# Expert weights in slots of two row blocks of four experts, instead of one expert per slot

## The chip, the cores and the metric

The kernel runs on one core of a Trainium2 chip. The metric is the device time of one execution in microseconds (us). Times inside an execution come from a hardware profile of one execution and count from its first instruction.

## The reference

One decoder layer over 256 tokens of width 1024: four token mixers (attention, indexer attention, gated linear attention, RWKV-7) merged by gates, a layer norm, and a mixture of 32 experts in 4 groups, two experts for each token. The part that the change touches is the mixture:

```python
hg = jnp.einsum('sd,edh->seh', xs, w_gate)     # w_gate, w_up: 32 x 1024 x 256
hu = jnp.einsum('sd,edh->seh', xs, w_up)
h = jax.nn.silu(hg) * hu * gate[..., None]     # gate is 0 but for two experts of a token
return jnp.einsum('seh,ehd->sd', h, w_down)    # w_down: 32 x 256 x 1024
x = _layer_norm(DN_ALPHA * x + y, ln_g[l, 1], ln_b[l, 1])
```

All of it is float32. The three expert matrices are 96 loads of 1 MB.

## The kernel before

The layer is one program, unrolled. Its first part (mixers, merge, output projection, router) is written as generators, and the string `ORDER` says by hand, letter by letter, which generator takes its next step. Letters of its last stretch: `O` output projection, `Q` and `R` norm and router of token blocks 0 and 1, `Y` and `Z` their normalised rows, `E` the gather for the first experts, `L` one weight load. Each engine runs its instructions in the order in which the program issues them.

The experts are worked in 8 groups of four (`g`, NQUAD = 8). Up to 32 tokens of each expert are gathered by a matmul with a selection matrix, so that four experts with 32 columns each fill the 128 columns of TensorE. For a group: gate products (`mwg`), `way_back` (two transposes of the selection matrix), up products (`mwu`), gather for the next group (`ahead`), SiLU on ScalarE and VectorE (`hh`), two transposes (`ph`, copied to `hT`), down products (`down`, from `mwd`), a copy to SBUF (`dn_copy`), and `back`, which adds the rows into the four accumulators `yacc` of PSUM. Groups 6 and 7 do their down products at the end of the program, as their `mwd` comes last in `stream`.

All loads go through the queue of SyncE in the order of `stream`: for groups 0 to 5 four `mwg`, four `mwu`, four `mwd`; then `mwg` and `mwu` of 6 and 7; then `mwd` of 6 and of 7. A load (`fetch`) takes a slot of 8 KB in each of 128 partitions, in a cycle of NL = 25 (two of each 25 are made of two half slots, with two loads of half the size). The first 25 are issued by the letters `L`, the others where `wload` first asks for them, and each waits on SyncE until its slot is free. In the kernel before, a slot holds one expert's whole matrix: `[P, 8 row blocks, 256]` for gate and up, `[P, 2, 1024]` for down. The product loop runs over row blocks `k` outside and the four experts inside, so that it touches all four slots from its first step to its last. A float32 matmul here shows as two MATMUL instructions.

The last 8 loads (`mwd` of 6 and 7) are cut: group 6 into row halves of 512 KB, group 7 into pieces of 256 KB by column half and row half (`tails`). At the end the gain and bias rows of the second layer norm are spread over all partitions by matmuls (`spread`, 32 instructions) between the two halves of the down products of group 6; then come `down` of 7, `last_copy`, `last_back`, the moments, the norm, and four stores.

If a token overflows an expert's 32 places (`flag`), a branch at the end computes everything densely; it is jumped over here.

Of the kernel before, what the change touches and what calls it, by code (L numbers as in the profile page):

```python
# [113 lines left out]
def _layout(inp):  # L114
# [35 lines left out]
    o["wout"] = g["w_out"][0].reshape(KT // 2, 2, P, D).transpose(0, 2, 1, 3)  # L150
    o["mwg"] = g["moe_w_gate"][0].reshape(NEXP, KT, P, HID).transpose(0, 2, 1, 3)
    o["mwu"] = g["moe_w_up"][0].reshape(NEXP, KT, P, HID).transpose(0, 2, 1, 3)
    o["mwd"] = g["moe_w_down"][0].reshape(NEXP, 2, P, D).transpose(0, 2, 1, 3)
    pc = np.zeros((P, NPC), f)
# [66 lines left out]
    "CPSMPSCMCDPLDPPPSMCSPSMNPSMPPNPSPCMMNMPMPSNSPCXLLMSMMMNNPPMPLMSPMMSMSMLPLPPMLNMLSPPMSSNPMSMMPMNMMPSS"  # L221
    "PPLLSPPMMMMMMMMPNSMPPMMSUUUUPUUPPMMMOUULMMMMLMMLOUMUMLOUUOUULLLMOUUOULUOQOOQQQQQQQRQQLQQOQLQLRRRYQQQ"
    "QQRSYLRQRRUQRRRRQRRZQZRQRRRRERLRRRRLLREQEQEREL"
)


def body(ctx, tc, I, out):
# [16 lines left out]
    def slot(name, shape, dt=F32):  # L244

        n = int(np.prod(shape[1:]))
        if n > 1024:
            return view(rp.tile([P, 2048], dt, tag="w2", bufs=NW, name=name), n, shape)
        return view(rp.tile([P, 1024], dt, tag="w", bufs=NS, name=name), n, shape)
# [997 lines left out]
    for g in range(NQUAD + 1):  # L1247
        if g < NQUAD:
            stream += [(src, 4 * g + e, [P, KT, HID]) for src in ("mwg", "mwu") for e in range(4)]

        if g != NQUAD - 2:
            for j in ((NQUAD - 2, NQUAD - 1) if g == NQUAD else (g,) if g < NQUAD - 2 else ()):
                stream += [("mwd", 4 * j + e, [P, 2, D]) for e in range(4)]
    fetched, tails = [], []

    def fetch():
        n = len(fetched)
        src, e, shape = stream[n]
        cyc = n % NL
        if cyc >= NL - NS // 2:  # L1260

            m = shape[1] // 2
            h = [slot("w", [P, m, shape[2]]) for _ in range(2)]
            ds = [(h[i], I[src][e][:, m * i:m * i + m]) for i in range(2)]
            at = lambda k: h[k // m][:, k % m]
        else:
            t = view((MP["rb"] if cyc < NR else rp).tile([P, 2048], F32, tag="w2", bufs=NR if cyc < NR else NW, name="w2"), 2048, shape)
            ds = [(t, I[src][e])]
            at = lambda k: t[:, k]
        fetched.append(at)  # L1270
        if n < len(stream) - 8:
            for d, a in ds:
                SY.dma_start(d, a)
            return

        tails.extend((k, at(k), I[src][e][:, k]) for k in range(2))
        if n % 4 == 3:
            for hs in (slice(0, 512), slice(512, 1024)) if n == len(stream) - 1 else (slice(0, 1024),):
                for _, d, a in sorted(tails, key=lambda x: x[0]):
                    SY.dma_start(d[:, hs], a[:, hs])  # L1280
            tails.clear()

# [255 lines left out]
    def down(g, k, h, pd):  # L1538
        for e4 in range(4):
            T.matmul(pd[h][32 * e4:32 * e4 + 32], lhsT=outs[g][0][:, k, 32 * e4:32 * e4 + 32], rhs=wds[g][e4](k)[:, 512 * h:512 * h + 512],  # L1540
                     start=k == 0, stop=k == 1, tile_position=(0, 32 * e4))
# [14 lines left out]
    def back(g, h, dn):  # L1556
        for q in range(2):
            T.matmul(yacc[q, h], lhsT=outs[g][1][:, q], rhs=dn[h], start=False, stop=False, skip_group_check=True)  # L1558

    idA = sq_([P, P], "idA", bufs=1)  # L1560
    G.tensor_scalar(idA, ident, ALPHA, None, op0=OP.mult)
    for g in range(NQUAD):
# [4 lines left out]
        for i, src in enumerate(("mwg", "mwu")):  # L1567
            ws = [wload() for _ in range(4)]
            for k in range(KT):
                for e4 in range(4):  # L1570
                    T.matmul(pgu[32 * e4:32 * e4 + 32, i], lhsT=xg[:, k, 32 * e4:32 * e4 + 32], rhs=ws[e4](k),  # L1571
                             start=k == 0, stop=k == KT - 1, tile_position=(0, 32 * e4))
            if i == 0:
                SGT = way_back(g)
                if more:
                    for q in range(2):
                        select(g + 1, q)
# [14 lines left out]
        V.scalar_tensor_tensor(hh, in0=hh, scalar=1.0, in1=pgu[:, 0], op0=OP.add, op1=OP.mult)  # L1592
        V.scalar_tensor_tensor(hh, in0=hh, scalar=0.5, in1=pgu[:, 1], op0=OP.mult, op1=OP.mult)
        ph = ps([P, 2, P])
        for k in range(2):
# [16 lines left out]
        if g < NQUAD - 2:  # L1612
            pd = downs(g)
            for k in range(2):
                for h in range(2):
                    down(g, k, h, pd)
# [34 lines left out]
    def scaled(q, h, src, dst):  # L1651

        hs = slice(512 * h, 512 * h + 512)
        V.scalar_tensor_tensor(dst[:, hs], in0=src, scalar=mvs[q][:, 0:1], in1=g2[:, hs], op0=OP.subtract, op1=OP.mult)  # L1654

    def normed(q, h, dst):
        hs = slice(512 * h, 512 * h + 512)
        V.scalar_tensor_tensor(dst[:, hs], in0=dst[:, hs], scalar=mvs[q][:, 2:3], in1=b2[:, hs], op0=OP.mult, op1=OP.add)  # L1658
        SY.dma_start(out[128 * q:128 * q + 128, hs], dst[:, hs])
# [3 lines left out]
    pd = downs(g)  # L1663
    for k in range(2):
        for h in range(2):
            down(g, k, h, pd)
        if k == 0:

            g2, b2 = twin("ln2", [P, D])
            for i, t in (("ln_g2", g2), ("ln_b2", b2)):  # L1670
                for h in range(2):
                    p = ps([P, 512])
                    spread(i, h, False, p)
                    A.copy(t[:, 512 * h:512 * h + 512], p)
    for h in range(2):
        dn_copy(dn, pd, h)
    for h in range(2):
        back(g, h, dn)
# [3 lines left out]
    def last_copy(h):  # L1682
        A.copy(dn[h], pd[h])
# [12 lines left out]
    for h in range(2):  # L1696
        down(g, 0, h, pd)
        if h:
            for q in range(2):
                first_half(q)  # L1700
        down(g, 1, h, pd)
        last_copy(h)
    for q in range(2):
# [8 lines left out]
    A.activation(res[0][:, h0], yacc[0, 0], AF.Identity, scale=mv[:, 2:3], bias=mv[:, 3:4])  # L1712
    G.tensor_tensor(res[0][:, h0], res[0][:, h0], g2[:, h0], op=OP.mult)
    G.tensor_tensor(res[0][:, h0], res[0][:, h0], b2[:, h0], op=OP.add)
    scaled(0, 1, yacc[0, 1], res[0])
# [11 lines left out]
    with tc.If(flag > 0):  # L1727
# [8 lines left out]
        for k in range(KT):  # L1736
# [3 lines left out]
            A.activation(xo[k // 4][:, k % 4, :], f2(pt), AF.Identity, scale=pcol("ln_g", k), bias=pcol("ln_b", k))  # L1740
        with tc.For_i(0, NEXP, 1) as e:
            wg, wu, wd_ = (slot("wo", sh) for sh in ([P, KT, HID], [P, KT, HID], [P, 2, D]))
            for t, n in ((wg, "mwg"), (wu, "mwu"), (wd_, "mwd")):
                SY.dma_start(t, I[n][bass.ds(e, 1)][0])
            hx = slot("hx", [P, 2, S])
            pg = ps([P, 2, S])
            pu2 = ps([P, 2, S])
            for c in range(2):
                for k in range(KT):
                    T.matmul(pg[:, c], lhsT=wg[:, k, 128 * c:128 * c + 128], rhs=xo[k // 4][:, k % 4, :], start=k == 0, stop=k == KT - 1)  # L1750
            for c in range(2):
                for k in range(KT):
                    T.matmul(pu2[:, c], lhsT=wu[:, k, 128 * c:128 * c + 128], rhs=xo[k // 4][:, k % 4, :], start=k == 0, stop=k == KT - 1)
            A.activation(hx, pg, AF.Tanh, scale=0.5)
            V.scalar_tensor_tensor(f2(hx), in0=f2(hx), scalar=1.0, in1=f2(pg), op0=OP.add, op1=OP.mult)
            V.scalar_tensor_tensor(f2(hx), in0=f2(hx), scalar=0.5, in1=f2(pu2), op0=OP.mult, op1=OP.mult)
            for q in range(2):
                for h in range(2):
                    pd_ = ps([P, 512], pj)
                    for k in range(2):  # L1760
                        T.matmul(pd_, lhsT=hx[:, k, 128 * q:128 * q + 128], rhs=wd_[:, k, 512 * h:512 * h + 512], start=k == 0, stop=k == 1)
                    hs = slice(512 * h, 512 * h + 512)
                    V.scalar_tensor_tensor(acc[q][:, hs], in0=pd_, scalar=gcur[:, q, 0:1], in1=acc[q][:, hs], op0=OP.mult, op1=OP.add)
            gtmp = sq_([P, 2, 32], "gtmp")
            V.tensor_copy(gtmp[:, :, 0:31], gcur[:, :, 1:32])
            V.tensor_copy(gcur[:, :, 0:31], gtmp[:, :, 0:31])
        for q in range(2):
# [22 lines left out]
```

## Time and profile before

| | us |
|---|---|
| median of 3 runs | 500.91 |
| lowest and highest of the 3 | 498.99, 501.34 |
| profiled execution, its own time | 499.01 |
| its span, first to last instruction | 497.2 |

The span is 1.8 us shorter than the time of the same execution. In it TensorE's matmuls are busy for 454.9 us (91%), VectorE for 237.7 us, ScalarE for 192.2 us, and the queue of SyncE moves 146.11 MB. Matmuls are pipelined and counted from start to modelled end, so "busy" is not peak. PE is TensorE's matmuls, PEld its weight loads, DVE VectorE, ACT ScalarE, POOL GpSimd, SPq the queue of SyncE. L1571 is line 1571 of the kernel. A row "x64" merges 64 instructions. PEclk is the granted share of TensorE's full clock (1.00 is 2.4 GHz, 0.50 is 1.2 GHz).

### The profile page before, as it was taken

The page shows a single profiled execution, that of the slowest core. Times are in us where ns is not written, and L with a number is a line of the kernel's source. Part 1 is how long each engine was busy: PE and PEld are TensorE (multiplying, and loading weights), DVE is VectorE, ACT ScalarE, POOL GpSimd, SP SyncE. Part 2 cuts the span into 40 slices and gives each one's busy share as a digit, 9 for nine tenths or more (in the row PEclk, how much of TensorE's full clock was granted, in tenths as well). Part 3 has the DMA queues.
Part 4 walks back from the last instruction along what each step waited for, and adds up shares of the span by engine and source line. Part 5 has one row for each costly group of instructions (what it writes and reads, how often), then busy time and mean ns, then how long its engine had stood idle before and what let it go on. Part 6 is the DMA issues. An engine that isn't in the chain of part 4 may idle for free. (4 is left out here: it accounts for less than half of the span.)

```text
span 497.2 us, 9471 instructions
## 1 busy us (share of the span) xinstructions
PE 454.9 (91%) x3968; PEld 333.9 (67%) x3968; DVE 237.7 (48%) x487; ACT 192.2 (39%) x353; POOL 49.9 (10%) x52
## 2 busy tenths in 40 slices
PE   7999999999999999999999899998988989876891
PEld 5989898998777888888878776563544536352520
DVE  4568648988987556657664643021212212120015
ACT  5767656353684965344453341010202012010311
POOL 1101112510100004333050000000000000000002
PEclk8899999999999999999999989999999999998897
DMA  8977522222242256699999999999999999999942
GB/s 275 395 330 272 196 86 87 86 88 86 86 171 86 86 181 225 266 426 420 356 407 390 354 371 421 420 397 424 415 420 422 418 422 415 421 420 415 394 170 88
DMA packets 27557, 146.74 MB, mean 295 GB/s; under 512 B 3124, under 2 KB 5752, under 8 KB 12536
## 3 DMA queue, kind: packets, MB, share of 16 engines
q1 hardware_dynamic: 27512, 146.11, 74.7%
q8 instruction: 32, 0.52, 0.4%
q14 instruction: 13, 0.11, 0.1%
HBM read 143.48 MB, written 2.62 MB: 294 GB/s over the span
## 5 line engine op out<-in xcount | busy, mean ns | idle before, releaser
L374 DVE TENSOR_TENSOR hl<-w,hl 128x1024 fp32r<-128x1024 f32 (+1 forms) x75 | 90.3, 1221 | 41.3 <-ACT hl L373 41.3
L373 ACT CAST hl<-w 128x1024 fp32r<-128x1024 f32 (+1 forms) x75 | 74.1, 1014 | 19.8 <-PE ps L390 12.4
L1571 PE MATMUL ps<-w,xg 128*32 128x256 f32 x1024 | 65.6, 396 | 7.6 <-DMA w<-mwu 5.8
L388 PE MATMUL ps<-hl,xh 128*128 128x512 f32 (+1 forms) x160 | 60.3, 377 | 0.0
L390 PE MATMUL ps<-hl,xh 128*128 128x512 f32 (+1 forms) x160 | 58.9, 368 | 0.0
L389 PE MATMUL ps<-hl,xl 128*128 128x512 f32 (+1 forms) x160 | 58.9, 368 | 0.0
L1571 PEld LDWEIGHTS ps<-w,xg 128*32 128x32 f32 x1024 | 33.7, 114 | 37.2 <-issue 8.5
L388 PE MATMUL ps<-xl,hl 128*128 128x256 f32 x160 | 48.7, 304 | 2.9 <-ACT hl L373 2.3
L389 PE MATMUL ps<-xh,hl 128*128 128x256 f32 x160 | 46.9, 293 | 0.1
L390 PE MATMUL ps<-xh,hl 128*128 128x256 f32 x160 | 46.4, 290 | 0.0
L388 PEld LDWEIGHTS ps<-xl,hl 128*128 128x128 f32 x160 | 32.0, 200 | 6.4 <-ACT hl L373 2.5
L1473 PE MATMUL ps<-Sel,nrm 128*128 128x128 f32 x256 | 33.6, 287 | 1.2 <-DVE smr L1437 0.7
L1473 PEld LDWEIGHTS ps<-Sel,nrm 128*128 128x128 f32 x256 | 31.3, 200 | 4.3 <-issue 3.7
L388 PEld LDWEIGHTS ps<-hl,xh 128*128 128x128 f32 x160 | 30.1, 188 | 5.7 <-issue 0.6
L390 PEld LDWEIGHTS ps<-hl,xh 128*128 128x128 f32 x160 | 30.1, 188 | 5.1
L389 PEld LDWEIGHTS ps<-hl,xl 128*128 128x128 f32 x160 | 30.2, 189 | 5.0 <-issue 0.2
L389 PEld LDWEIGHTS ps<-xh,hl 128*128 128x128 f32 x160 | 31.9, 199 | 0.9 <-DVE hl L374 0.7
L1558 PE MATMUL ps<-small,SGT 128*128 128x512 f32 x48 | 23.7, 616 | 9.3 <-DVE small L1552 5.1
L390 PEld LDWEIGHTS ps<-xh,hl 128*128 128x128 f32 x160 | 31.9, 199 | 0.0
L1523 ACT COPY SGT<-ps 128x256 f32<-128x256 f32 x8 | 3.0, 373 | 69.0 <-PE ps L1521 69.0
L1552 DVE COPY small<-ps 128x512 f32<-128x512 f32 x6 | 4.2, 692 | 51.4 <-PE ps L1558 51.4
L1540 PE MATMUL ps<-w,small 128*32 128x512 f32 x192 | 23.1, 598 | 3.5 <-ACT xg L1480 3.0
(405 smaller groups left out, 667.1 us busy)
## 6 DMA issues: line engine op xcount, KB each, us to landing
w<-mwu SPq DMA_DIRECT2D x32, 1024.0 KB, 15.0
w<-mwg SPq DMA_DIRECT2D x27, 1024.0 KB, 15.2
w<-win SPq DMA_DIRECT2D x26, 1024.0 KB, 7.0
w<-mwd SPq DMA_DIRECT2D x23, 1024.0 KB, 14.2
w<-mwd SPq DMA_DIRECT2D x10, 512.0 KB, 13.7
w<-mwg SPq DMA_DIRECT2D x10, 512.0 KB, 15.4
w<-wbr SPq DMA_DIRECT2D x4, 1024.0 KB, 5.7
w<-wout SPq DMA_DIRECT2D x4, 1024.0 KB, 7.4
```

Source lines behind the costliest of these rows:

```text
L373: A.copy(hi, src)
L374: V.tensor_tensor(lo, src, hi.bitcast(F32), op=OP.subtract)
L388: T.matmul(dst, lhsT=ls[0], rhs=rs[1], start=start, stop=False)
L389: T.matmul(dst, lhsT=ls[1], rhs=rs[0], start=False, stop=False)
L390: T.matmul(dst, lhsT=ls[0], rhs=rs[0], start=False, stop=stop)
L1473: T.matmul(pg[:, k4], lhsT=nrm[q][:, 128 * k:128 * k + 128], rhs=f2(SelR[g, q]), start=q == 0 and k4 == 0, stop=True, skip_group_check=True)
L1523: A.copy(SGT, pg)
L1540: T.matmul(pd[h][32 * e4:32 * e4 + 32], lhsT=outs[g][0][:, k, 32 * e4:32 * e4 + 32], rhs=wds[g][e4](k)[:, 512 * h:512 * h + 512], start=k ...
L1552: V.tensor_copy(dn[h], pd[h])
L1558: T.matmul(yacc[q, h], lhsT=outs[g][1][:, q], rhs=dn[h], start=False, stop=False, skip_group_check=True)
L1571: T.matmul(pgu[32 * e4:32 * e4 + 32, i], lhsT=xg[:, k, 32 * e4:32 * e4 + 32], rhs=ws[e4](k), start=k == 0, stop=k == KT - 1, tile_position ...
```

## The change

A slot of gate or up weights now holds two of the eight row blocks of all four experts of a group (`[P, 2, 4, 256]`), and a slot of down weights one row block and one column half of all four experts (`[P, 4, 512]`, slot number 2 h + k). The host lays the arrays out so that a slot is still 8 KB in one piece for each partition. The product loop asks for a new slot with each second `k`. The cut of the last 8 loads is gone: they are whole slots. The down products run by column half `h` first, then `k`, with copy and `back` after each column half for groups 6 and 7. The spread of the gain rows moves into group 7, between its SiLU and its transposes; that of the bias rows comes after the first of four down steps of group 6. The end of `ORDER` is rewritten from its 572nd letter on. The overflow branch goes over four experts in one turn of its loop.

```diff
-    o["mwg"] = g["moe_w_gate"][0].reshape(NEXP, KT, P, HID).transpose(0, 2, 1, 3)
-    o["mwu"] = g["moe_w_up"][0].reshape(NEXP, KT, P, HID).transpose(0, 2, 1, 3)
-    o["mwd"] = g["moe_w_down"][0].reshape(NEXP, 2, P, D).transpose(0, 2, 1, 3)
+    for n, k in (("mwg", "moe_w_gate"), ("mwu", "moe_w_up")):
+        o[n] = g[k][0].reshape(NQUAD, 4, 4, 2, P, HID).transpose(0, 2, 4, 3, 1, 5).reshape(NEXP, P, 2, 4, HID)
+    o["mwd"] = g["moe_w_down"][0].reshape(NQUAD, 4, 2, P, 2, 512).transpose(0, 4, 2, 3, 1, 5).reshape(NEXP, P, 4, 512)
...
-    "PPLLSPPMMMMMMMMPNSMPPMMSUUUUPUUPPMMMOUULMMMMLMMLOUMUMLOUUOUULLLMOUUOULUOQOOQQQQQQQRQQLQQOQLQLRRRYQQQ"
-    "QQRSYLRQRRUQRRRRQRRZQZRQRRRRERLRRRRLLREQEQEREL"
+    "PPLLSPPMMMMMMMMPNSMPPMMSUUUUPUUPPMMMOUULMMMMLMMLOUMUMLOUUOUULLLMOUUOULULOQLOOQQQQOQQRQQQQQRRRQRRRSQY"
+    "LRQRQRQRRQQYRZQLLQQQRRQELZRRRRLRRURLRRQEERRQEE"
...
-        if n < len(stream) - 8:
-            for d, a in ds:
-                SY.dma_start(d, a)
-            return
-
-        tails.extend((k, at(k), I[src][e][:, k]) for k in range(2))
-        if n % 4 == 3:
-            for hs in (slice(0, 512), slice(512, 1024)) if n == len(stream) - 1 else (slice(0, 1024),):
-                for _, d, a in sorted(tails, key=lambda x: x[0]):
-                    SY.dma_start(d[:, hs], a[:, hs])
-            tails.clear()
+        for d, a in ds:
+            SY.dma_start(d, a)
...
-            T.matmul(pd[h][32 * e4:32 * e4 + 32], lhsT=outs[g][0][:, k, 32 * e4:32 * e4 + 32], rhs=wds[g][e4](k)[:, 512 * h:512 * h + 512],
+            T.matmul(pd[h][32 * e4:32 * e4 + 32], lhsT=outs[g][0][:, k, 32 * e4:32 * e4 + 32], rhs=wds[g][2 * h + k](e4),
...
+    gb = []
+
+    def ln2(i, pool):
+
+        if not gb:
+            gb.extend(twin("ln2", [P, D]))
+        for h in range(2):
+            p = ps([P, 512], pool)
+            spread(("ln_g2", "ln_b2")[i], h, False, p)
+            A.copy(gb[i][:, 512 * h:512 * h + 512], p)
...
-            ws = [wload() for _ in range(4)]
             for k in range(KT):
+                if k % 2 == 0:
+                    w = wload()
                 for e4 in range(4):
-                    T.matmul(pgu[32 * e4:32 * e4 + 32, i], lhsT=xg[:, k, 32 * e4:32 * e4 + 32], rhs=ws[e4](k),
+                    T.matmul(pgu[32 * e4:32 * e4 + 32, i], lhsT=xg[:, k, 32 * e4:32 * e4 + 32], rhs=w(k % 2)[:, e4],
...
+        if not more:
+            ln2(0, pj)
         ph = ps([P, 2, P])
...
-    for k in range(2):
-        for h in range(2):
-            down(g, k, h, pd)
-        if k == 0:
-
-            g2, b2 = twin("ln2", [P, D])
-            for i, t in (("ln_g2", g2), ("ln_b2", b2)):
-                for h in range(2):
-                    p = ps([P, 512])
-                    spread(i, h, False, p)
-                    A.copy(t[:, 512 * h:512 * h + 512], p)
     for h in range(2):
+        down(g, 0, h, pd)
+        if h == 0:
+
+            ln2(1, px)
+        down(g, 1, h, pd)
         dn_copy(dn, pd, h)
-    for h in range(2):
         back(g, h, dn)
...
     for h in range(2):
-        down(g, 0, h, pd)
-        if h:
+        for k in range(2):
+            down(g, k, h, pd)
+        last_copy(h)
+        if h == 0:
             for q in range(2):
                 first_half(q)
-        down(g, 1, h, pd)
-        last_copy(h)
...
-        with tc.For_i(0, NEXP, 1) as e:
+        with tc.For_i(0, NEXP, 4) as g:
```

## Rows read from the trace of the kernel before

**Rows 1.** The page: clock, DMA share and rate in 40 slices of 12.4 us

```profile
PEclk8899999999999999999999989999999999998897
DMA  8977522222242256699999999999999999999942
GB/s 275 395 330 272 196 86 87 86 88 86 86 171 86 86 181 225 266 426 420 356 407 390 354 371 421 420 397 424 415 420 422 418 422 415 421 420 415 394 170 88
```

**Rows 2.** The queue of SyncE in order of time: start us, us

```profile
430.87 7.79 SPq L1273 DMA_DIRECT2D w<-mwu  x4
...
461.90 2.88 SPq L1280 DMA_DIRECT2D w<-mwd  x3
...
470.20 2.31 SPq L1280 DMA_DIRECT2D w<-mwd  x4
...
473.98 1.38 SPq L1280 DMA_DIRECT2D w<-mwd  x3
```

**Rows 3.** DMA issues from 474.4 us on: count, KB, median us to landing

```profile
w<-mwd SPq DMA_DIRECT2D x3, 256.0 KB, 4.7
```

**Rows 4.** The chain of waits from 456 us on: start us, us, what

```profile
438.33 20.93 DMA w<-mwu
...
459.31 5.34 PE ps L1571 x58
...
466.11 0.41 PE ps L1596 x2
466.52 1.85 PE ps L1540 x16
468.38 3.81 PE ps L1529 x32
...
474.05 3.63 PE ps L1558 x8
477.68 2.71 PE ps L1540 x24
480.39 1.91 PE ps L1686 x4
482.30 1.12 PE ps L1540 x8
...
483.44 0.59 ACT dn L1683
```

**Rows 5.** Stretches: us, busy us of each engine (instructions), PEclk, DMA share, GB/s

```profile
436.00:440.00 4.00, 2.12 (x34) 1.07 (x36) 0.00 (x0) 0.00 (x0) 0.00 (x0) 1.00 1.01 422
...
456.00:460.00 4.00, 1.31 (x17) 0.57 (x21) 0.00 (x0) 0.00 (x0) 0.00 (x0) 1.00 1.00 405
460.00:464.00 4.00, 4.00 (x48) 2.06 (x41) 0.00 (x0) 0.00 (x0) 0.00 (x0) 0.57 1.03 410
...
480.00:484.00 4.00, 3.30 (x16) 0.83 (x12) 1.40 (x2) 0.82 (x2) 0.00 (x0) 1.00 0.00 0
```

**Rows 6.** TensorE in order of time from 318 us on

```profile
322.93 3.66 PE L1571 MATMUL ps<-w,xg 128*32 128x256 f32 x64
```

**Rows 7.** The same view as rows 5, earlier stretches

```profile
276.00:280.00 4.00, 3.76 (x27) 3.15 (x25) 2.77 (x5) 1.40 (x5) 0.00 (x0) 1.00 0.86 303
280.00:284.00 4.00, 3.11 (x25) 2.54 (x23) 2.98 (x14) 2.11 (x5) 0.00 (x0) 1.00 0.95 320
...
328.00:332.00 4.00, 4.00 (x61) 2.82 (x54) 0.84 (x2) 0.38 (x1) 0.00 (x0) 1.00 0.91 356
```

**Rows 8.** The queue of SyncE, two earlier stretches: start us, us

```profile
276.55 3.69 SPq L1273 DMA_DIRECT2D w<-mwu  x2
...
326.60 1.28 SPq L1273 DMA_DIRECT2D w<-mwg  x3
```

**Rows 9.** Waits of that queue, 318 to 328 us: total us, times, longest

```profile
SPq L1273 <- PE ps L1521: 8.0, 1, 8.0
```

**Rows 10.** The branch over the overflow part: ns min/median/max, start us

```profile
L1727 SPq COMPARE_BRANCH  x1: 45/45/45, 494.9 to 494.9; - x1
```

More of the change, by code (lines that the diff above doesn't have):

```diff
@@ L1248, in body @@
         if g < NQUAD:
-            stream += [(src, 4 * g + e, [P, KT, HID]) for src in ("mwg", "mwu") for e in range(4)]
+            stream += [(src, 4 * g + e, [P, 2, 4, HID]) for src in ("mwg", "mwu") for e in range(4)]
         if g != NQUAD - 2:
             for j in ((NQUAD - 2, NQUAD - 1) if g == NQUAD else (g,) if g < NQUAD - 2 else ()):
-                stream += [("mwd", 4 * j + e, [P, 2, D]) for e in range(4)]
-    fetched, tails = [], []
+                stream += [("mwd", 4 * j + e, [P, 4, 512]) for e in range(4)]
+    fetched = []
     def fetch():
@@ L1262, in fetch @@
             m = shape[1] // 2
-            h = [slot("w", [P, m, shape[2]]) for _ in range(2)]
+            h = [slot("w", [P, m] + shape[2:]) for _ in range(2)]
             ds = [(h[i], I[src][e][:, m * i:m * i + m]) for i in range(2)]
@@ L1613, in body @@
             pd = downs(g)
-            for k in range(2):
-                for h in range(2):
+            for h in range(2):
+                for k in range(2):
                     down(g, k, h, pd)
@@ L1653, in scaled @@
         hs = slice(512 * h, 512 * h + 512)
-        V.scalar_tensor_tensor(dst[:, hs], in0=src, scalar=mvs[q][:, 0:1], in1=g2[:, hs], op0=OP.subtract, op1=OP.mult)
+        V.scalar_tensor_tensor(dst[:, hs], in0=src, scalar=mvs[q][:, 0:1], in1=gb[0][:, hs], op0=OP.subtract, op1=OP.mult)
     def normed(q, h, dst):
         hs = slice(512 * h, 512 * h + 512)
-        V.scalar_tensor_tensor(dst[:, hs], in0=dst[:, hs], scalar=mvs[q][:, 2:3], in1=b2[:, hs], op0=OP.mult, op1=OP.add)
+        V.scalar_tensor_tensor(dst[:, hs], in0=dst[:, hs], scalar=mvs[q][:, 2:3], in1=gb[1][:, hs], op0=OP.mult, op1=OP.add)
         SY.dma_start(out[128 * q:128 * q + 128, hs], dst[:, hs])
@@ L1663, in body @@
     pd = downs(g)
-    for k in range(2):
-        for h in range(2):
-            down(g, k, h, pd)
-        if k == 0:
-            g2, b2 = twin("ln2", [P, D])
-            for i, t in (("ln_g2", g2), ("ln_b2", b2)):
-                for h in range(2):
-                    p = ps([P, 512])
-                    spread(i, h, False, p)
-                    A.copy(t[:, 512 * h:512 * h + 512], p)
     for h in range(2):
+        down(g, 0, h, pd)
+        if h == 0:
+            ln2(1, px)
+        down(g, 1, h, pd)
         dn_copy(dn, pd, h)
-    for h in range(2):
         back(g, h, dn)
@@ L1696, in body @@
     for h in range(2):
-        down(g, 0, h, pd)
-        if h:
+        for k in range(2):
+            down(g, k, h, pd)
+        last_copy(h)
+        if h == 0:
             for q in range(2):
                 first_half(q)
-        down(g, 1, h, pd)
-        last_copy(h)
     for q in range(2):
@@ L1712, in body @@
     A.activation(res[0][:, h0], yacc[0, 0], AF.Identity, scale=mv[:, 2:3], bias=mv[:, 3:4])
-    G.tensor_tensor(res[0][:, h0], res[0][:, h0], g2[:, h0], op=OP.mult)
-    G.tensor_tensor(res[0][:, h0], res[0][:, h0], b2[:, h0], op=OP.add)
+    G.tensor_tensor(res[0][:, h0], res[0][:, h0], gb[0][:, h0], op=OP.mult)
+    G.tensor_tensor(res[0][:, h0], res[0][:, h0], gb[1][:, h0], op=OP.add)
     scaled(0, 1, yacc[0, 1], res[0])
@@ L1740, in body @@
             A.activation(xo[k // 4][:, k % 4, :], f2(pt), AF.Identity, scale=pcol("ln_g", k), bias=pcol("ln_b", k))
-        with tc.For_i(0, NEXP, 1) as e:
+        with tc.For_i(0, NEXP, 4) as g:
             wg, wu, wd_ = (slot("wo", sh) for sh in ([P, KT, HID], [P, KT, HID], [P, 2, D]))
-            for t, n in ((wg, "mwg"), (wu, "mwu"), (wd_, "mwd")):
-                SY.dma_start(t, I[n][bass.ds(e, 1)][0])
             hx = slot("hx", [P, 2, S])
[L1746 to L1763, printed above, removed]
@@ new lines, in body @@
+            pg, pu2 = (ps([P, 2, S]) for _ in range(2))
+            for e in range(4):
+                for j in range(4):
+                    for t, n in ((wg, "mwg"), (wu, "mwu")):
+                        SY.dma_start(t[:, 2 * j:2 * j + 2], I[n][bass.ds(g, 4)][j][:, :, e])
+                    SY.dma_start(wd_[:, j % 2, 512 * (j // 2):512 * (j // 2) + 512], I["mwd"][bass.ds(g, 4)][j][:, e])
+                for c in range(2):
+                    for k in range(KT):
+                        T.matmul(pg[:, c], lhsT=wg[:, k, 128 * c:128 * c + 128], rhs=xo[k // 4][:, k % 4, :], start=k == 0, stop=k == KT - 1)
+                for c in range(2):
+                    for k in range(KT):
+                        T.matmul(pu2[:, c], lhsT=wu[:, k, 128 * c:128 * c + 128], rhs=xo[k // 4][:, k % 4, :], start=k == 0, stop=k == KT - 1)
+                A.activation(hx, pg, AF.Tanh, scale=0.5)
+                V.scalar_tensor_tensor(f2(hx), in0=f2(hx), scalar=1.0, in1=f2(pg), op0=OP.add, op1=OP.mult)
+                V.scalar_tensor_tensor(f2(hx), in0=f2(hx), scalar=0.5, in1=f2(pu2), op0=OP.mult, op1=OP.mult)
+                for q in range(2):
+                    for h in range(2):
+                        pd_ = ps([P, 512], pj)
+                        for k in range(2):
+                            T.matmul(pd_, lhsT=hx[:, k, 128 * q:128 * q + 128], rhs=wd_[:, k, 512 * h:512 * h + 512], start=k == 0, stop=k == 1)
+                        hs = slice(512 * h, 512 * h + 512)
+                        V.scalar_tensor_tensor(acc[q][:, hs], in0=pd_, scalar=gcur[:, q, e:e + 1], in1=acc[q][:, hs], op0=OP.mult, op1=OP.add)
@@ L1764, in body @@
             gtmp = sq_([P, 2, 32], "gtmp")
-            V.tensor_copy(gtmp[:, :, 0:31], gcur[:, :, 1:32])
-            V.tensor_copy(gcur[:, :, 0:31], gtmp[:, :, 0:31])
+            V.tensor_copy(gtmp[:, :, 0:28], gcur[:, :, 4:32])
+            V.tensor_copy(gcur[:, :, 0:28], gtmp[:, :, 0:28])
         for q in range(2):
```

## Prediction

> **What bounds the kernel now.** I read the page's 40 slices first. From about 211 us on the rate stands near 420 GB/s in most slices [rows 1], and from 299 us it hardly leaves it: the transfers of the expert weights set the pace, and an engine that gets faster there wins nothing by itself. Two things can still be had: time in which the transfers stand still, and what follows the last ones. So I read the end, in the chain of waits [rows 4]. The last load of up weights lands at 459.27 us. From there to the copy at 483.44 us the chain has no transfer in it: it is TensorE's work in order, with short steps of ScalarE and VectorE. Yet 8 MB of down weights are still under way. Their last issue starts a little before 475.0 us [rows 2] and lands some 4.7 us later [rows 3], at about 479.7 us; after 480 us nothing moves [rows 5]. The last down products begin at 482.30 us [rows 4], 2.6 us after their data is there. So the last 24 us are bound by TensorE, closely followed by the transfers; any gain there ends where the transfers take over.
>
> **Part 1: the tail from the landing L of the last up load.** Before, almost a whole pass of 64 instructions begins at L: 58 of them, 5.34 us, up to 464.65 us [rows 4]. The other six found their data earlier, as each load is one expert. They are slow, too: the granted clock of 460 to 464 us is 0.57, a mixture of 1.2 and 2.4 GHz, after four microseconds with only 1.31 us of matmuls [rows 5]; at 1.00 a pass of 64 takes 3.66 us [rows 6]. With slots of two row blocks, three quarters of the pass are done when L comes. Left are 16 instructions: a quarter of 3.66 us is 0.9, and about 0.3 for the last to drain: L+1.2.
>
> Then I lay out the new order with the durations of rows 4. Spread of the gain rows, half of 3.81: to L+3.1. It costs TensorE nothing for the first 1.46 us, as SiLU runs on ScalarE and VectorE then (from 464.65 to 466.11 us before). Transposes 0.41, then ScalarE must finish the second spread copy (0.59, the size of the copy at 483.44 us) before it copies hT: down products start at L+4.2. Down step 0.93 (half of 1.85), spread of the bias rows 1.9, down step 0.93, copy 0.65 with its hand-over, back 1.82 (half of 3.63), two down steps 1.85, VectorE's copy 0.75, back 1.82: L+14.9. Group 7: two down steps 1.81 (two thirds of 2.71), copy 0.65, back 1.91, a step 0.9, the last step 1.12: L+21.2. In this new order two copies stand in TensorE's way that did not before, together 1.4 us; the sum has them. Before, the same point (483.42) is L+24.15. TensorE's chain is 2.9 us shorter.
>
> Do the transfers allow it? Whole slots at 422 GB/s [rows 5] take 1,048,576 B / 422 GB/s = 2.49 us each; eight end at L+19.9 = 479.2 us instead of 479.7. The small difference is that the cut loads ran slower: 410 GB/s at 460 us [rows 5], 394 in the slice from 460 us [rows 1]. The last step needs the whole last slot now, where it could begin on 256 KB before: 479.2 + 1.15 = 480.4, so transfers allow 3.1 us. The smaller, 2.9 us, holds. The seven other slots land at L+2.5, L+5.0 and so on, each before its step in the list above, so no further wait enters.
>
> **Part 2: slots come free earlier.** Before, the four gate slots of a group are free only when its pass ends. This stopped the queue for 8.0 us until way_back of group 1 [rows 9], the next loads went out at 326.60 us [rows 8], and in 328 to 332 us the transfers were busy for 0.91 of the time [rows 7]: 0.09 x 4 = 0.36 us lost. The pass starts at 322.93 us [rows 6]; its first slot would be free a quarter pass later, at about 323.9, nearly 3 us sooner. I take 0.4 us; bounds 0 (another slot late instead) and 0.5. After 332 us the queue is full, issues following landings every 2.49 us (430.87 us, four in 7.79) [rows 2], so earlier free slots there give nothing: a load lands 20.93 us after its issue [rows 4], some eight loads of 2.49 us, and these cover it.
>
> **Part 3: the new order.** Its loads 17 and 18, counted from 0, and others are issued between earlier steps; SyncE's queue holds little else there, so the place counts by the slot it gets. In 276 to 284 us transfers are idle for 0.14 x 4 + 0.05 x 4 = 0.76 us [rows 7], where two loads went out 3.4 us apart [rows 8]. All of it could be filled: 0.8 at most. On the other side, if one load slips by one such step, 3.4 less the 2.49 that one load covers is 0.9 lost. I take a gain of 0.4. If the router starts the experts later by up to about 3 us, the earlier first slot covers it.
>
> **Costed at nothing.** Issues fall by 16 (24 cut pieces become 8 loads); the queue waits for landings there anyway. A semaphore wait for each slot instead of four at once lies beside waits for data. Host layout and overflow branch are outside the path; the longer code is only jumped over, SyncE's branch being 45 ns at 494.9 us [rows 10]. No row shows whether a farther jump costs more: nothing to 0.5 us, taken as nothing, nearest to that row.
>
> **Sum.** 2.9 + 0.4 + 0.4 = 3.7 us off the profiled execution: 499.01 - 3.7 = 495.3. That execution stands 1.9 us below the median of 500.91 and beside the lowest run, 498.99. No row says which the changed kernel's median will resemble, so I add half, 0.95: **496.2 us**.
>
> **Where a rule speaks against the change.** The row first: after the four microseconds with 1.31 us of matmuls the clock was at 0.57, after other short bursts (436 us, 2.12 us of 4) it was 1.00 [rows 5]. The change turns each pass into four bursts of about 1 us, one for each landing, 2.49 us apart, so bursts of either kind are possible. The Trainium skill, "TensorE: Matmul & The Clock Gate", section "HAM oscillation — how this bites in real kernels", describes short bursts between waits for transfers that leave each burst on the low clock, and advises running all K tiles before waiting for data. By that rule the old slots would be the better ones; the trace agrees in the burst at 459.31 us, but that one belongs to the old slots. While transfers set the pace a burst at 1.2 GHz, about 2 us, still ends before the next landing, so only the tail pays.
>
> **The rivals.**
>
> *One low stretch in the tail.* If the clock falls once near L, as it did at 460 us before, the quarter pass takes 0.9 us longer and the spread behind it about 0.7: the tail gains 2.9 - 1.6 = 1.3, with the rest 2.1: 499.01 - 2.1 + 0.95 = 497.9. For it: rows 5 show it in this place. Against: there are twice as many matmuls before L now.
>
> *All gaps close.* Part 2 gives 0.5, part 3 gives 0.8, and the rate of the slices from 273 to 298 us (354 and 371 against 421 [rows 1]) rises in part, some 1 us: 5.2 in all, 494.8. Against: at a busy share of 0.86 the full rate would be 0.86 x 422 = 363, and 303 was measured [rows 5, 7], so that busy transfers were slow there too, which slots don't mend.
>
> *The loads slip.* The new order loses 0.9 where I gave 0.4, and the low stretch comes too: 1.3 + 0.4 - 0.9 = 0.8; 499.2, no change that can be told.
>
> *Slower: the clock stays low.* TensorE works for some 18 of the 21 us after L; each microsecond of it at 1.2 GHz does half its work. The 3.7 us of gain are lost after 7.4 us at 1.2 GHz, and after 12.4 us the kernel is slower by 2.5 us; at 1.2 GHz throughout it would lose some 18 - 3.7 = 14 us: 514. For it: bursts like those of rows 5. Against: the slice from 472 us, deep in the tail before, stands at nine tenths [rows 1], and the new tail is as dense after its first steps.
>
> **Chances.** Forecast 0.54, own range 494.7 to 497.5; one low stretch 0.20; all gaps close 0.12; loads slip 0.08; clock stays low 0.06. A measurement here tells some 0.5% (2.5 us) from no change: below 498.4 counts as faster. Of the forecast nine tenths, of the low stretch a little over half, and all of the third are faster: 0.49 + 0.11 + 0.12 = 0.72; 0.21 the same; 0.07 slower. Range: the low end takes most of the third case with tails to 493.2, the high end the second and fourth to 499.4.
>
> **What the profile after will show.** The chain of waits should have about 16 instructions of the up products after the last up load instead of 58; the last landing should lie 1 us or less before the last down step, where it was 2.6; the last copy should begin near L+21.2. The share in 328 to 332 us should be near 1.00, and the last up load land near 458.5 us. Wrong would be: a last landing clearly later than L+20, PEclk near 0.5 in the slices after L, or L itself later than 459.3, which would mean that the new order lost time ahead of the experts.

## The result

| | before | after |
|---|---|---|
| median, us | 500.72 (20 runs) | 497.24 (20 runs) |
| profiled execution, us | 499.01 | 495.77 |
| its span, us | 497.2 | 493.9 |

The ratio over the fast runs (one of the 20 runs before took 1561 us) is 0.9938, 95% interval 0.9921 to 0.9955: 0.6% faster. The medians are 3.5 us apart. Predicted were 496.2 us and a range of 493.2 to 499.4. Both profiled executions lie below the median of their kernel, by 1.7 us before and by 1.5 us after.

The total was met; its parts were not. Along the path to the end, the 3.3 us between the two spans split up so:

| stretch | before | after | change |
|---|---|---|---|
| start to the first load of the output projection's weights (same code) | 226.55 | 225.80 | -0.75 |
| from there to L, the landing of the last up load | 232.72 | 230.95 | -1.77 |
| L to the last copy | 24.17 | 21.10 | -3.07 |
| last copy to the issue of the last store | 9.39 | 9.62 | +0.23 |
| that issue to the end | 4.37 | 6.43 | +2.06 |

L is the landing of the last up load. The first three rows scatter from one execution to the next: where the code up to L is that of before (the long-branch kernel below), the second row took 235.60 us, and in a second profile of the changed kernel the second and third took 232.15 and 21.66. The last row is the steady one: 4.3 to 4.6 us in the eleven profiles with a short gap at the jump (below), 6.4 to 6.7 in the three with a long one.

**The tail.** The chain of waits of the kernel after, from 456 us on (start us, us, what), which answers to [rows 4]:

```profile
456.80 1.07 PE ps L1576 x16
457.87 1.98 PE ps L1522 x16
459.85 0.22 PE ps L1603 x2
460.06 1.00 PE ps L1533 x8
461.06 1.98 PE ps L1522 x16
463.04 1.04 PE ps L1533 x8
464.11 0.59 ACT dn L1547
...
464.74 1.98 PE ps L1551 x4
466.73 1.90 PE ps L1533 x16
...
471.38 1.90 PE ps L1533 x16
...
475.92 1.90 PE ps L1533 x16
477.85 0.59 ACT dn L1683
```

L is 456.75 us. Behind it stand 16 up instructions (L1576), where 58 stood; then the spreads (L1522) and the down steps (L1533) in the new order. The last copy begins at 477.85, L+21.1.

The stretches of the same kernel (columns as in [rows 5]):

```profile
292.00:296.00 4.00, 4.00 (x70) 1.99 (x66) 2.30 (x15) 2.50 (x9) 0.00 (x0) 1.00 1.03 416
296.00:300.00 4.00, 4.00 (x67) 2.53 (x60) 0.35 (x2) 0.43 (x2) 0.00 (x0) 1.00 1.03 424
328.00:332.00 4.00, 4.00 (x48) 3.42 (x37) 1.91 (x6) 0.76 (x2) 0.00 (x0) 1.00 1.00 414
...
452.00:456.00 4.00, 3.31 (x32) 0.99 (x24) 0.00 (x0) 0.00 (x0) 0.00 (x0) 0.55 1.01 420
456.00:460.00 4.00, 3.21 (x38) 2.46 (x35) 0.84 (x2) 1.09 (x3) 0.00 (x0) 1.00 1.02 424
```

The gap at 328 us is closed: share 1.00, where [rows 7] has 0.91. From 292 to 300 us the rate is 416 and 424 GB/s. The clock does fall in this kernel, but from 448.8 to 455.6 us, ahead of L; from 456 to 480 us the tail has 1.00.

**The jump.** The branch over the overflow part (columns as in [rows 10]; the last row counts from SyncE's first instruction behind it):

```profile
L1727 PEldq COMPARE_BRANCH  x1: 3662/3662/3662, 479.5 to 479.5; - x1
...
L1727 SPq COMPARE_BRANCH  x1: 45/45/45, 489.5 to 489.5; - x1
...
L1727 SPq EVENT_SEMAPHORE  x8: 17/17/17, 492.0 to 492.5; - x8
```

SyncE branches at 489.45 us, and its next instruction comes at 491.98: 2.53 us. Before, the two were 0.50 us apart. TensorE's own branch takes 3662 ns, where it took 373; TensorE has nothing more to do by then. The same rows before, with SyncE's branch in [rows 10]:

```profile
L1727 SPq EVENT_SEMAPHORE  x7: 17/17/17, 495.4 to 495.8; - x7
L1727 PEldq COMPARE_BRANCH  x1: 373/373/373, 485.1 to 485.1; - x1
```

The branch instruction itself still takes 45 ns on SyncE: the time is behind it. In that time, 489.55 to 491.9 us, the trace of after has a single transfer, 8 KB from 490.42 to 490.74 us on a queue that the profile calls instruction (packets, MB, share of 16 engines):

```profile
q14 instruction: 1, 0.01, 0.9%
```

Before, SyncE's next instruction comes ahead of such a transfer, which begins 1.06 us after the branch.

### The profile page after: what moved, and what is told of

It reads as the page before. It is cut to its first block, busy times and chain, and to the rows that moved or that the text cites. A ratio compares the mean times of both kernels' runs of the same rounds, so it can differ in the third digit from the quotient of the medians.

```text
span 493.9 us, 9468 instructions
## 1 busy us (share of the span) xinstructions
PE 451.3 (91%) x3968; PEld 330.6 (67%) x3968; DVE 237.7 (48%) x487; ACT 191.8 (39%) x353; POOL 49.5 (10%) x52
## 5 line engine op out<-in xcount | busy, mean ns | idle before, releaser
L375 ACT CAST hl<-w 128x1024 fp32r<-128x1024 f32 (+1 forms) x75 | 74.1, 1014 | 19.1 <-PE ps L392 12.4
L1576 PE MATMUL ps<-w,xg 128*32 128x256 f32 x1024 | 64.0, 398 | 8.5 <-DMA w<-mwu 6.4
L1576 PEld LDWEIGHTS ps<-w,xg 128*32 128x32 f32 x1024 | 31.7, 113 | 38.6 <-DMA w<-mwu 11.1
L391 PE MATMUL ps<-xh,hl 128*128 128x256 f32 x160 | 46.3, 289 | 0.3 <-DVE hl L376 0.2
L392 PE MATMUL ps<-xh,hl 128*128 128x256 f32 x160 | 45.9, 287 | 0.0
L391 PEld LDWEIGHTS ps<-xh,hl 128*128 128x128 f32 x160 | 31.4, 196 | 0.9 <-DVE hl L376 0.8
L392 PEld LDWEIGHTS ps<-xh,hl 128*128 128x128 f32 x160 | 31.3, 196 | 0.0
L1551 PEld LDWEIGHTS ps<-small,SGT 128*128 128x128 f32 x48 | 8.2, 189 | 24.6 <-DVE small L1545 10.1
```

The source lines that it names most:

```text
L375: A.copy(hi, src)
L391: T.matmul(dst, lhsT=ls[1], rhs=rs[0], start=False, stop=False)
L392: T.matmul(dst, lhsT=ls[0], rhs=rs[0], start=False, stop=stop)
```

## The experiments

Each kernel was timed beside the kernel before on the same chip; the 12 ran in three batches (jobs), in which the kernel before had medians of 500.35, 499.56 and 498.89 us. A ratio is always to that, so kernels of different jobs are compared by ratio. "w0" is the issue of the first load of the output projection's weights, from which on the code of the kernels differs; "load 27" counts the weight loads from 0.

### A short overflow branch

One expert's products in the program text again, in a loop of four within the loop over groups; the rest as after:

```diff
         with tc.For_i(0, NEXP, 4) as g:
...
-            for e in range(4):
+            with tc.For_i(0, 4, 1) as e:
...
```

> The changed kernel, with the overflow branch as a loop of four inside a loop of eight (12 loads and one expert's products in the text instead of 48 loads and four experts'). Theory J (the jump over the longer branch costs 2.0 us at the end): the gap on SyncE from its branch instruction to the next falls from 2.53 us to about 0.5, the last copy stays near L+21.1, span some 492, ratio near 0.990. Rival (the longer end of the changed kernel is chance or belongs to the stores): gap stays above 2 us, ratio stays 0.994.

Measured: 494.93 us, ratio 0.9887 (0.985 to 0.9923). Its rows of the branch:

```profile
L1727 SPq EVENT_SEMAPHORE  x8: 17/17/17, 492.0 to 492.5; - x8
L1727 PEldq COMPARE_BRANCH  x1: 373/373/373, 481.5 to 481.5; - x1
...
L1727 SPq COMPARE_BRANCH  x1: 45/45/45, 491.5 to 491.5; - x1
```

SyncE goes on 0.49 us after its branch, TensorE's takes 373 ns. The profiled span is the same 493.9 us as that after, though: what the jump gives back, this execution loses at L. The chain of waits at that place:

```profile
457.19 1.94 PE ps L1576 x16
459.13 2.69 PE ps L1522 x16
```

Both steps take longer than after (1.07 and 1.98), as the clock is at 0.50 from 453.7 to 460.6 us, and the last copy begins at L+22.7.

### A long branch in the kernel before

The loads of the overflow branch are cut into 16 pieces each, 48 instead of 3, with the products left as they were:

```diff
-                SY.dma_start(t, I[n][bass.ds(e, 1)][0])
+                for k in range(t.shape[1]):
+                    m = t.shape[2] * t.shape[1] // 16
+                    for c in range(0, t.shape[2], m):
+                        SY.dma_start(t[:, k, c:c + m], I[n][bass.ds(e, 1)][0][:, k, c:c + m])
```

> The kernel before, with nothing changed but the loads of its overflow branch, which is jumped over: each cut into 16 pieces, 48 in the text of the loop instead of 3; the products of the branch stay as they are. Theory J, and that SyncE's own length counts: the gap after SyncE's branch rises from 0.50 to about 2.5 us, all else stays, ratio near 1.004. Rival K (the length on TensorE or the other engines counts): gap 0.5, ratio 1.000.

Measured: 501.45 us, ratio 1.0025 (1.0003 to 1.0047), and these rows:

```profile
L1727 SPq EVENT_SEMAPHORE  x8: 17/17/17, 497.5 to 498.0; - x8
L1727 PEldq COMPARE_BRANCH  x1: 373/373/373, 485.1 to 485.1; - x1
...
L1727 SPq COMPARE_BRANCH  x1: 45/45/45, 495.0 to 495.0; - x1
```

SyncE's gap is 2.51 us with the old products, TensorE's branch still 373 ns. So SyncE pays for its own part of the skipped text, and TensorE doesn't pay for SyncE's. The median moved by 1.1 us of the 2.0 in the profile; the interval holds both.

### The short branch with the old ORDER, and the new ORDER alone

The first is the kernel with the short branch and the `ORDER` of before, the second the kernel before with the `ORDER` of after (the same diff backwards):

```diff
-    "...OULULOQLOOQQQQOQQRQQQQQRRRQRRRSQY" "LRQRQRQRRQQYRZQLLQQQRRQELZRRRRLRRURLRRQEERRQEE"
+    "...OULUOQOOQQQQQQQRQQLQQOQLQLRRRYQQQ" "QQRSYLRQRRUQRRRRQRRZQZRQRRRRERLRRRRLLREQEQEREL"
```

> As e1_small_branch, with the ORDER of the kernel before. Theory S (the last up load lands 2.5 us earlier because slots come free earlier, and the new order gives nothing): landing L within 0.4 us of e1's, ratio within 0.001 of e1's. Rival O (the new order gives it): L 0.8 us or more later than in e1_small_branch, ratio 0.002 or more higher.

> The kernel before with the new ORDER and nothing else. Theory O (the new order gives 0.7 to 1.4 us, as e3 beside e1 suggests): load 23, counted from 0, lands 0.7 us or more earlier, counted from the first wout issue; ratio 0.997 to 0.9985. Rival S (it gives nothing in old slots): ratio 1.000.

Measured: the old ORDER 496.13 us, 0.9914 (0.9887 to 0.9941), against 0.9887 with the new one, 1.2 us in that job; the new ORDER alone 498.61 us, 0.9983 (0.9957 to 1.0009), a median 0.95 us below before. L came 1.4 us later after w0 with the old ORDER than with the new one (233.1 against 231.7). In the first expectation these are the rival's numbers, and in the second the ratio is the theory's. But the two intervals of the first pair overlap, and that of the second run holds 1. The profiles point the same way on average: load 23, which no early slot can have helped, lands 68.2, 69.6, 69.9 and 70.4 us after w0 in the four profiles with the old order, mean 69.5, and 67.9 to 70.2, mean 68.8, in the ten with the new one. The pair alone doesn't show it: in the run with the new ORDER alone load 23 landed at 68.5, and 68.2 is the kernel before.

### The new gate and up slots alone

The kernel before with the new slots for gate and up and a branch of the short form; down slots, cut of the last loads, tail and ORDER are the old ones:

```diff
-            ws = [wload() for _ in range(4)]
             for k in range(KT):
+                if k % 2 == 0:
+                    w = wload()
```

> The kernel before with the new slots for gate and up weights alone: old ORDER, old down weights with the cut last loads, old place of the spread (the branch loops as in e1_small_branch). Theory: from L the chain is 24.15 less 4.1 = 20.0 us, but the cut down loads land some 20.4 us after L, and the last step ends about L+21.6; L lies some 2 us earlier than before; ratio 0.990 to 0.992, so that the other parts of the change add next to nothing. Rival (the moved spread and the column halves give a good part of the tail): ratio 0.994 or more, last copy at L+22.5 or later.

Measured: 497.66 us, ratio 0.9947 (0.9926 to 0.9969), 2.7 us faster. Not in the tail: the last copy begins at L+24.3 (24.2 before). The chain there:

```profile
460.80 0.66 PE ps L1597 x2
461.46 4.64 PE ps L1540 x16
466.10 4.25 PE ps L1529 x32
470.35 1.85 PE ps L1540 x16
```

The up pass ends 2.0 us after L (457.3 us), but the first down step, 1.85 us in [rows 4], takes 4.64: it waits for the cut loads of group 6, at a clock of 0.50 (456.7 to 467.0 us). Half speed is some 1.85 of the 2.79 us that it takes longer, the wait the rest, so how the old order of the tail would do at the full clock isn't shown. The 2.7 us would then lie ahead of L, but the profiles don't tell it from scatter: from w0 to L this one took 232.5 us, the kernel before 232.7, and the long-branch kernel 235.6.

Time and tail are the rival's of the expectation, and so is a comparison within the job: the kernel with the short branch and the old ORDER (496.13 us) differs from this one by the new down slots and tail alone, and is 1.5 us faster.

### The new tail without the new gate and up slots

The kernel with the short branch, gate and up slots of one expert each:

```diff
+            ws = [wload() for _ in range(4)]
             for k in range(KT):
-                if k % 2 == 0:
-                    w = wload()
```

> As e1_small_branch, with gate and up slots of one expert as before; all else of the change stays (whole down slots, column halves, moved spreads, new ORDER). Theory B (bursts before L and early slots are most of the gain): the pass of 58 or more instructions begins at L again and takes 3.5 us at the full clock, 5.3 at half, against 1.1 to 1.9 in e1; last copy at L+24.5 to L+26; ratio 0.996 to 1.001. Rival (the down slots and the new order carry the gain): last copy at L+23 or sooner, ratio 0.992 or less.

Measured: 499.67 us, ratio 1.0006 (0.9988 to 1.0024). The 58 up instructions stand behind L again:

```profile
457.88 5.53 PE ps L1575 x58
```

From their end to the last copy it takes 19.98 us where it took 18.79 [rows 4]: the new tail is 1.2 us longer by itself. The medians agree: beside the kernel with the new ORDER alone in the same job (498.61 us), this one is 1.1 us slower. Its gain hangs on the new slots.

### Slots held to the end of the pass

The kernel with the short branch; in groups 0 to 6, or in 1 to 6 alone (the last line, in place of the second), the row blocks are taken in an order that uses the first slot of a pass first and last:

```diff
-            for k in range(KT):
+            ks = (0, 2, 4, 6, 7, 5, 3, 1) if more else range(KT)
...
+            ks = (0, 2, 4, 6, 7, 5, 3, 1) if more and g else range(KT)
```

> As e1_small_branch, but in groups 0 to 6 the row blocks of a pass go 0, 2, 4, 6, 7, 5, 3, 1, so that the first slot is held until the pass ends; starts and instruction counts stay, group 7 is unchanged. Theory S (early free slots give about 1 us between 296 and 335 us): the load issued after the 25 first ones goes out 2.5 to 3 us later than in e1 and L lies 0.8 to 2 us later, ratio 0.002 to 0.004 above e1. Rival (eight loads in flight cover it): L and ratio as e1 within 0.001.

> The kernel with the short overflow branch, the row blocks of groups 1 to 6 in the order 0,2,4,6,7,5,3,1, which holds the first slot of each pass to its end; only group 0 gives its slots back early. Theory F (the whole gain of earlier slots comes from the first slot that is freed at all, while all slots are full): load 27 lands 75.1 us after the first issue of the output projection's weights, L 231 to 232 after it, median as the kernel without the edit in the same job, within 0.6 us. Rival (each group's earlier slots add a little): load 27 at 75.1 all the same, but L at 233 or later and the median 1.5 us slower, as in the run where groups 0 to 6 all hold their first slot.

Measured: groups 0 to 6 496.55 us, 0.9936 (0.991 to 0.9961); groups 1 to 6 alone 494.30 us, 0.9917 (0.9887 to 0.9946), beside 494.45 us, 0.9913 (0.9884 to 0.9943), for the kernel without the edit in the same job. Stretches with the slots of groups 0 to 6 held:

```profile
292.00:296.00 4.00, 3.16 (x56) 1.34 (x48) 1.69 (x10) 2.10 (x8) 0.00 (x0) 1.00 1.00 384
296.00:300.00 4.00, 4.00 (x70) 2.18 (x66) 0.49 (x2) 0.37 (x1) 0.00 (x0) 1.00 0.81 285
```

and without the edit, in the last job:

```profile
292.00:296.00 4.00, 4.00 (x69) 2.18 (x67) 2.85 (x16) 2.17 (x8) 0.00 (x0) 1.00 1.01 385
296.00:300.00 4.00, 4.00 (x74) 2.18 (x66) 0.49 (x2) 0.37 (x1) 0.00 (x0) 1.00 1.03 423
```

In group 0's first pass all 25 slots are full. Held, the first comes free 3.7 us after the pass began, and the queue runs dry; given back after a quarter, 1.1 us. So the gain lies in group 0, as far as the medians show: with it alone giving slots early, 0.15 us separate them, though six runs of each leave room for about 1 us. One caution: in the profile of that run, group 0's pass began some 2 us late after w0 (67.8 us; 65.5 to 65.9 in the other three of the job), behind a clock of 0.50 from 281.9 to 292.1 us, and load 27 landed no earlier than with held slots (76.8 us after w0; 75.1 expected), and L came at 232.7 (231 to 232 expected). These rows went against the expectation; the time did not. The held order also makes the first pass wait 0.8 us for the second half of its gathered rows.

### Work in TensorE's gaps

The kernel with the short branch, and in the last group's gate and up passes, after each slot but the last, two added products, or one:

```diff
+        if not more:
+            fill = ps([P, 256], pj)
+            fills = csts[:, 0:256]
...
+                if not more and k % 2 and (i, k) != (1, KT - 1):
+                    for _ in range(2):
+                        T.matmul(fill, lhsT=ident, rhs=fills, start=True, stop=True)
```

> As e1_small_branch, with two extra products of 128x128 by 256 columns after each slot but the last of group 7's gate and up passes, into PSUM that nothing reads: they keep TensorE busy in its waits before L. Theory C (the clock at 1.2 GHz around L costs some 1.4 us in most runs): no stretch at 0.5 between L-3 and L+10, last copy at L+21.1, ratio 0.002 to 0.003 below e1. Rival (the extra products delay more than they save, or the clock falls all the same): last copy at L+22.5 or later, ratio as e1 or above.

> The changed kernel with the short overflow branch, and one added product without use (128x128 by 128x256) after each slot of the last group's gate and up passes but the last slot. The fill with two of them ended near where the kernel without fill did: its tail was at 1.00, but TensorE itself had become the pace from 437.9 us on, so that the last slot's products began 1.35 us after their landing. One product (0.53 us) in a slot step of 1.0 us leaves TensorE idle again before each landing. Theory C (the low clock across L costs some 1.4 us, and a little work in the gaps keeps it away): clock 1.00 from 441 to 484 us, last copy at L+21.0 to L+21.3, median 1 us below that of the kernel without fill in the same job, ratio near 0.986. Rival (so little work doesn't keep the clock, or what it gives back goes into the fill): last copy at L+22.3 to 22.7, median within 0.4 us of the kernel without fill.

Measured: two products 495.82 us, 0.9915 (0.9882 to 0.9947); one product 493.37 us, 0.9876 (0.9849 to 0.9904), 1.1 us below the kernel without fill in the same job. With two the clock is 1.00 from 441.0 to 485.4 us, but from 437.9 us on the chain is TensorE alone, the last up product ends 2.3 us after L, and the last copy begins at L+22.3. With one the clock is 1.00 from 441.3 to 485.7 us and the last copy begins at L+21.1. Stretches with one product, and then without, in the same job:

```profile
452.00:456.00 4.00, 3.05 (x36) 1.17 (x28) 0.00 (x0) 0.00 (x0) 0.00 (x0) 1.00 1.02 426
456.00:460.00 4.00, 3.37 (x38) 2.60 (x42) 0.84 (x2) 1.25 (x3) 0.00 (x0) 1.00 1.01 422
```

```profile
452.00:456.00 4.00, 2.92 (x28) 0.99 (x28) 0.00 (x0) 0.00 (x0) 0.00 (x0) 0.50 1.02 422
456.00:460.00 4.00, 3.23 (x38) 1.82 (x31) 0.62 (x2) 0.40 (x2) 0.00 (x0) 0.92 1.01 422
```

That the fill keeps the clock up is in the rows (both profiles with it have 1.00 from 441 us to the end of the tail, none of the seven without it that are counted below); that this is worth 1.1 us is not shown, as the intervals overlap and in this profile without fill, too, the low stretch ended (456.7 us) before L (457.7).

### The changed kernel again, beside the short branch

> The changed kernel as it is, beside the same kernel with the short branch on the same chip. Theory J (the longer overflow branch costs SyncE about 2.0 us at the jump): SyncE needs 2.5 us behind its branch, the ratio to the kernel before is 0.993 to 0.994, and the median stands 1.7 to 2.3 us above that with the short branch. Rival (the 0.5% between the two was chance, as their intervals overlapped): under 1 us between the medians.

> The changed kernel with the short overflow branch once more, as the base of the three others. Theory J: SyncE needs 0.5 us behind its branch, ratio 0.987 to 0.991. Rival: ratio 0.993, as with the long branch.

Measured: 497.63 us, 0.996 (0.9935 to 0.9985), and 494.45 us, 0.9913 (0.9884 to 0.9943). SyncE's gap is 2.78 us and 0.49, a difference of 2.3. The medians are 3.2 us apart, more than the 1.7 to 2.3 expected, and the ratio of the changed kernel lies above the 0.993 to 0.994 expected. The 0.9 us over are within the scatter, as the twelve runs of the changed kernel go from 493.05 to 500.07 us.

## Why the prediction was right, and where it was not

**The total was right because errors and luck cancelled.** Off the profiled execution 3.7 us were forecast and 3.3 measured. The jump took 2.06 us that were costed at nothing; parts 2 and 3 gave 1.77 instead of 0.8, part 1 gave 0.17 more; 0.75 came ahead of the changed code, which is luck; and 0.23 went between the last copy and the last store. The step that failed is in "Costed at nothing": the overflow branch "is only jumped over, SyncE's branch being 45 ns", "nothing to 0.5 us, taken as nothing". It costs 2.0 to 2.3 us of the gap, at the very end, where nothing hides it. The branch instruction was the nearest row, but the cost lies in the gap behind it, which the trace of before had, too, at 0.50 us, and which was not read.

**Part 1 (2.9 us predicted, 3.07 measured)** held in the profiled execution, with its working: 16 instructions, L+21.1 against L+21.2, the eight loads down to some L+19.9, the last of them about 0.2 us before the last down step. Inside, one step was wrong: the down products were to wait for ScalarE until L+4.2, but began at L+3.3, since group 6's need only group 6's hT; the longer pieces behind (backs 1.98 for 1.82 to 1.91, steps 1.00 to 1.04 for 0.93) took most of that up. That "two copies stand in TensorE's way that did not before, together 1.4 us", has its answer in the run without the new gate and up slots, whose tail is 1.2 us longer.

**One low stretch in the tail** was priced well (1.6 us) and given too small a chance (0.20). Of seven profiles with new slots, new tail and no fill, L to the last copy took 21.1 us in two, 21.7 in one and 22.5 to 22.7 in four, a loss of 1.4 to 1.6; all seven have a stretch at 0.50 between 431 and 462 us, and what counts is how much of it lies behind L: none in the two, 1.3 us in the one, 3.0 to 3.4 us in the four. The profiled execution was one of the two lucky ones. The mean of the seven is 22.0, that of the three profiles with the old slots and tail 24.3, so that part 1 is worth some 2.3 us on average. This bears on the Trainium skill, "TensorE: Matmul & The Clock Gate", section "HAM oscillation — how this bites in real kernels": bursts between landings do meet the low clock here, as it describes. Its advice to run all K tiles before waiting did not hold for the time: the run with the old slots had 58 instructions behind L at a clock of 0.50 and 0.78, and a ratio of 1.0006 (it lost the early slots, too, so the clock's share in that isn't shown), against 0.9887 and 0.9913 with the bursts.

**Part 2 (0.4 us) was mis-sized, and put in the wrong pass.** It read group 1, at 322 to 332 us, whose gap did close. The gain is in group 0, where 292 to 300 us ran at 371 and 377 GB/s in the kernel before and at 416 and 424 after, a difference of some 0.9 us at 422:

```profile
292.00:296.00 4.00, 4.00 (x70) 2.44 (x69) 2.74 (x14) 1.55 (x5) 0.00 (x0) 1.00 1.02 371
296.00:300.00 4.00, 4.00 (x74) 2.18 (x66) 0.49 (x2) 0.37 (x1) 0.00 (x0) 1.00 1.02 377
```

The DMA share of 1.02 doesn't show the queue dry, as a long packet counts as busy in it: from 65 to 78 us after w0, 14 packets of 8 KB took more than 500 ns before, and 2 after, where most take 309. What counts is when load 27, the first that needs a freed slot, goes out. In six profiles with early slots it did so 66.6 to 68.1 us after w0, and at most 4 packets were long; in the eight others (old slots, held slots, or a late group 0) at 69.4 to 70.9, with 8 to 31 long ones. By medians early slots are worth 1.2 to 2.4 us (ratios 0.9936 held, 0.9887 and 0.9913 not, in other jobs and with overlapping intervals) to 2.7 (gate and up slots alone). The rival "all gaps close" had this place and 1 us for it.

**Part 3 (0.4 us)** is about 1 us: 1.2 and 0.95 by medians, 0.7 by load 23, each uncertain by itself. The first job has all parts side by side, by medians: 500.35 us before, 497.66 with the new gate and up slots, 496.13 with the new down slots and tail, 494.93 with the new ORDER (all three with a short branch). These are 2.7, 1.5 and 1.2 us, 5.4 together, of which the long branch takes back 2 to 3.

**L and the median.** L came at 456.75, not 458.5; 0.75 of that was there before any changed code ran. Half of the distance between profiled execution and median was added; the whole was right, as 495.77 came with a median of 497.24.

**Open** is why the clock falls where it does. Its stretch at 0.50 between 282 and 295 us goes with a delay of group 0: its first pass begins 65.5 to 66.0 us after w0 in the eight profiles where the stretch lasts some 3 us, 66.7 to 67.2 in the three with some 7 us, and 67.8 to 68.0 in the three with some 10 us. In these last three load 27 went out at 69.4 to 69.6 in spite of early slots; the caution above is one of them. Whether the stretch causes the delay was not tried. Open, too, is what the one product of fill is worth.

The kernel with the short branch beats both, by 0.9% to 1.1% against before; with one product of fill the ratio was the lowest of all, 0.9876.

## What to carry to other kernels

Text that is only jumped over can have a price at the jump, for each engine by its own part of it, once that part is long enough: read the time from the branch to the engine's next instruction, and keep rare branches short with a loop. A slot that comes free a quarter pass earlier is worth most at the first pass behind a full ring, so look there before looking at the steady state. A total that comes out right says little: check every term, as here a hidden loss of 2 us stood against a gain that was sized too small.

## What the runs showed of the hardware that was not expected

SyncE's gap behind the branch was 0.50 us with 3 to 12 DMA issues in the skipped body (eleven profiles), and 2.51 to 2.78 with 48 (three profiles). From 3 to 12 it doesn't rise, so it is no price for each issue. TensorE's branch took 373 ns with one expert's products in the body and 3362 to 3662 ns with four.

In each of the three profiles with the long gap an 8 KB transfer of a queue that the profile calls instruction begins 0.9 to 1.2 us after SyncE's branch and ends 1.1 to 1.3 us before its next instruction. In the eleven others such a transfer begins 1.06 to 1.35 us after the branch, when SyncE has gone on already. TensorE's two long branches hold a 16 KB transfer of another instruction queue, 1.02 us after their start; behind its short ones it begins when they are over. So the engines look as if they waited for the text behind the jump to be loaded. No run here separates that from other causes.
